# Moving all gate projections of a hybrid decoder layer from the final merge into the RWKV phase

## The chip, the core and the metric

The kernel runs on one core of one Trainium2 chip. The metric is the device time of one execution in microseconds. The core has a matrix engine (TensorE, PE in the profile; its weight loads are listed as PEld), VectorE (DVE), ScalarE (ACT), GpSimd (POOL) and a queue engine (SyncE, SP) that issues most of the DMAs; ACT issues some too. The engines run their own instruction streams, each in a fixed order, and wait for each other by semaphores.

## The reference: what is computed

x is 2048 tokens of 1024 channels in float32; there is one layer and one sequence.

```
h = rms_norm(x, norm_pre)
proj = h @ w_in            # split into c_q, c_kv, k_rope | u_rwkv | g_q, g_k, g_v, g_lat | br_gate | merge_gate
y_mla  = mla_branch(...)   # causal softmax attention, 8 heads
y_rwkv = rwkv7_branch(...) # delta-rule recurrence, 8 heads of 64, in chunks
y_gla  = gla_branch(...)   # gated linear attention, 4 heads
ys     = stack([y_mla, y_rwkv, y_gla]) * silu(br_gate)          # (2048, 3, 512)
branch = einsum('bsnw,nwd->bsnd', ys, w_branch_out)             # (2048, 3, 1024)
merged = sum(sigmoid(merge_gate) * branch, over the 3 branches) # (2048, 1024)
x      = x + rms_norm(merged @ w_out, norm_post)
```

br_gate has 3 × 512 channels and merge_gate 3 × 1024. Together they are 4608 channels, or 36 tiles of 128, each a product of h with a 1024 × 128 slice of w_in. These 36 gate tiles are what the change moves. Gates 0 to 11 are br_gate (four tiles for each branch), gates 12 to 35 are merge_gate (eight for each branch).

## The kernel before

**Arithmetic.** Data lie with channels on the 128 partitions and tokens along the free side, in blocks of 512 tokens (`TB`), four blocks in all (`NB`). A large product in fp32 is made from three fast matmuls: each operand is split into a high part (a cast to fp32r) and a low part (the rest), and `mm3` (lines 133 to 140) adds high·high, high·low and low·high into PSUM. One output tile of 128 channels by 512 tokens from 1024 inputs thus takes 8 × 3 = 24 matmuls. A weight comes as four loads of 128 KB; each load is split by a cast on ACT (line 121) and a subtraction on POOL (line 122), in `load_w` and `split`.

**RWKV phase** (`phase_rwkv`, line 331). For each block the kernel normalises x, transposes it into h (high and low, 16 tiles in a single buffer) and projects from it. The recurrence is cut into 16 stages (two channel groups × two half blocks × four blocks). A stage has a triangular solve on VectorE with round trips through DRAM (`within`), a preparation (`prepare`), and a chain of four chunk steps (`chain`) in which TensorE, VectorE and ACT alternate. The projections are filler for TensorE between these steps: `project_group` issues, for each half of a block's channels, its RWKV tiles (13 a block, `mixed`) and the tiles that the two other mixers need later (12 a block, `plain`, which go to the DRAM tensor `more` by `Plain.run`, lines 309 to 321). `mm3` records its matmuls in a list while `k.filling` is set, and `place` (line 142) ties the steps of `prepare` and `chain` to positions spread evenly over that list.

The instructions of each engine are ordered by a planner that simulates the program. Its priorities are program positions; `tc.high_priority(offset=PRI)` and its like put the recurrence ahead of the filler by so many instructions (`PRI` for chain and preparation, `PRI_W` for the solve, `PRI_O` for the operands, `PRI_H` for the next block's h).

**The fourth block's gates.** The last two stages have no later block to project. There `spare` (lines 1460 to 1464) makes all 36 gate tiles of the fourth block from its h, with a priority far behind everything (`PRI_LOW`), and stores them to the DRAM tensor `early`. They also fill TensorE while the GLA phase runs.

**GLA and MLA phases** (`phase_gla`, `phase_mla`) read `more`, and write y_g and y_m to DRAM; y_r is written by the RWKV phase.

**Merge** (`phase_merge`, line 1250). It goes through two halves of 1024 tokens. For each half it loads x again, normalises it with the known factors and transposes it into h (only the first 512 tokens in the second half, since the gates of the fourth block are known). For each of the three branches, in the order MLA, RWKV, GLA, it then projects the four br_gate tiles, forms y · silu(gate) and splits it into `yh` and `yl` (line 1312); and for each pair of output tiles it projects the merge_gate tiles, multiplies `yh`/`yl` by w_branch_out into `psb`, and adds tanh-gated results into `mg` (lines 1337 and 1340). The gate weights are loaded and split in each half anew. At the end comes the product with w_out and the last norm, 16 row tiles of 128 tokens, with the w_out halves in the places of h.

The lines that change in the merge are these two kinds of projection:

```
                    w = gate(n * 4 + i)
...
                            pre = project(b, w)
...
                        w = gate(12 + n * 8 + d)
...
                            pre = th if known(b) else project(b, w)
```

Of the kernel before, what the change touches and what calls it, by code (L numbers as in the profile page):

```python
# [9 lines left out]
F32 = mybir.dt.float32  # L10
F32R = mybir.dt.float32r
# [7 lines left out]
S = 2048  # L19
D = 1024  # L20
# [301 lines left out]
PRI = 1500  # L322
PRI_W = 500
# [3 lines left out]
PRI_O = 500  # L327
# [3 lines left out]
def phase_rwkv(k, pl, x, pos, w_rwkv, w_up2, w_more, y_dram, more, rope_dram, spare):  # L331
# [4 lines left out]
    with ExitStack() as st:  # L336
# [46 lines left out]
        def plain(B, h, ns):  # L383
            sl = slice(B * TB, B * TB + TB)
            pl.run(h, [w_more[n_] for n_ in ns], [more[n_][:, sl] for n_ in ns])

# [326 lines left out]
        def project_group(i):  # L713
# [22 lines left out]
            m = w_more.shape[0] // 2  # L736
            if xs:
# [39 lines left out]
        for i in range(n):  # L777
# [470 lines left out]
XB = 3  # L1248
TH = 4
def phase_merge(k, x, ys, early, w_gate, w_br, w_o, n_post, out):  # L1250
# [5 lines left out]
    with ExitStack() as st:  # L1256
        pool = lambda name, bufs=1, **kw: st.enter_context(k.pool(name, bufs, **kw))
        hp = pool("me_h", side="right")
        xp = pool("me_x")
        wp = pool("me_w")  # L1260
        t1 = pool("me_t")
        per = pool("me_per")
        ps_m = pool("me_psm", 2, space=PSUM)
        ps_g = pool("me_psg", 3, space=PSUM)
        ps_b = pool("me_psb", 3, space=PSUM)
        npost = per.tile([128, D], F32, name="npost")
        mg = [per.tile([128, 8, T], F32, name=f"mg{u}") for u in range(S // T)]

        for half in range(S // T):
            t0 = half * T  # L1270

            def known(b):

                return t0 + b * TB == S - TB

            def project(b, w):
                ps = ps_g.tile([128, TB], F32, name="psg")
                k.project(ps, w, h, slice(b * TB, (b + 1) * TB))
                return ps
# [7 lines left out]
            if half == 0:  # L1287
                nc.scalar.dma_start(out=npost, in_=n_post)

            def gate(n):  # L1290
                return k.load_w8(wp, w_gate[n], 128, "w", parts=4, rb=3, hb=4)

            for n in range(3):
                yh = [per.tile([128, T], F32R, name=f"yh{i}") for i in range(4)]
                yl = [per.tile([128, T], F32R, name=f"yl{i}") for i in range(4)]
                for i in range(4):
                    w = gate(n * 4 + i)
                    yt = xp.tile([128, T], F32, name="h_x", bufs=XB)
                    nc.sync.dma_start(out=yt, in_=ys[n][i][:, t0:t0 + T])
                    for b in range(NT):  # L1300
                        sl = slice(b * TB, (b + 1) * TB)
                        if known(b):
                            pre = xp.tile([128, TB], F32, name="h_x", bufs=XB)
                            nc.sync.dma_start(out=pre, in_=early[n * 4 + i])
                        else:
                            pre = project(b, w)
                        th = t1.tile([128, TB], F32, name="th", bufs=TH)
                        nc.scalar.activation(out=th, in_=pre, func=AF.Tanh, scale=0.5)
                        nc.vector.scalar_tensor_tensor(out=th, in0=th, scalar=1.0, in1=pre, op0=ALU.add, op1=ALU.mult)
                        nc.vector.scalar_tensor_tensor(out=th, in0=th, scalar=0.5, in1=yt[:, sl], op0=ALU.mult,  # L1310
                                                       op1=ALU.mult)
                        k.split(yh[i][:, sl], yl[i][:, sl], th)

                for d0 in range(0, 8, 2):
                    gates = []
                    for d in (d0, d0 + 1):
# [174 lines left out]
```

## Time and profile before

| | |
|---|---|
| median of 3 runs | 3126.67 us (3118.32 to 3131.35) |
| the profiled execution | 3124.77 us, span 3123.0 us |
| mean granted TensorE clock | 0.969 |
| TensorE / VectorE / ACT / POOL busy | 95% / 58% / 44% / 52% |
| RWKV projections and other filler in the RWKV and GLA phases (`psd`) | 18.7 to 1506 us |
| transposes of the attention weights in MLA (`pst`, line 1177) | 1535 to 2068 us |
| gate projections in the merge (`psg`) | 2073 to 2930 us |
| product with w_out | 2940 to 3114 us |

The profile has a page, and views that cut the same trace by line, by tile, by wait and by time. Busy time of TensorE is the union of matmuls whose ends are modelled, and matmuls overlap; so a full TensorE is judged here by the number of matmuls in a stretch as well. PEclk is the granted share of its clock. In views that list groups, the columns are: line, engine, operation, output<-inputs, form, count | busy us, mean ns of one | idle time of the engine just before them, and what ended it.

### The profile page before, as it was taken

The page shows a single profiled execution, that of the slowest core. Times are in us where ns is not written, and L with a number is a line of the kernel's source. Part 1 is how long each engine was busy: PE and PEld are TensorE (multiplying, and loading weights), DVE is VectorE, ACT ScalarE, POOL GpSimd, SP SyncE. Part 2 cuts the span into 40 slices and gives each one's busy share as a digit, 9 for nine tenths or more (in the row PEclk, how much of TensorE's full clock was granted, in tenths as well). Part 3 has the DMA queues.
Part 4 walks back from the last instruction along what each step waited for, and adds up shares of the span by engine and source line. Part 5 has one row for each costly group of instructions (what it writes and reads, how often), then busy time and mean ns, then how long its engine had stood idle before and what let it go on. Part 6 is the DMA issues. An engine that isn't in the chain of part 4 may idle for free.

```text
span 3123.0 us, 53491 instructions
## 1 busy us (share of the span) xinstructions
PE 2967.1 (95%) x18048; PEld 2423.4 (78%) x18048; DVE 1801.9 (58%) x5194; ACT 1387.8 (44%) x3211; POOL 1620.0 (52%) x2198
## 2 busy tenths in 40 slices
PE   8899998999989998898999999989999999999998
PEld 6676776777767776666798998878888888888887
DVE  3668787686888745888588888861110103122443
ACT  3343433333334444566677777762222224334321
POOL 5745554564645556676545545433244446477422
PEclk9999999999989999889999999999999999999999
DMA  4323232323213333233200000142121213344322
GB/s 135 99 84 102 83 89 90 89 81 87 71 53 94 110 118 101 88 99 96 65 22 17 18 19 18 33 129 70 49 75 48 71 51 107 107 133 146 110 95 88
DMA packets 261091, 253.01 MB, mean 81 GB/s; under 512 B 75328, under 2 KB 228816, under 8 KB 260816
## 3 DMA queue, kind: packets, MB, share of 16 engines
q1 hardware_dynamic: 236048, 220.03, 23.6%
q10 hardware_dynamic: 24768, 29.55, 3.0%
q8 instruction: 143, 2.34, 0.3%
q14 instruction: 132, 1.08, 0.1%
HBM read 201.77 MB, written 47.71 MB: 80 GB/s over the span
## 4 chain that ended last, share of the span: by engine, by line
PE 77%; DVE 15%; DMA 4%; issue 2%; ACT 1%; POOL 1%; SPq 0%; DVEq 0%; ACTq 0%; POOLq 0%
PE psg L136 7%; PE psg L137 7%; PE psg L138 7%; PE psd L136 6%; PE psd L138 6%; PE psd L137 5%; PE pso L1199 4%; PE pst L1177 4%; PE psb L136 4%; PE psb L137 4%; PE psb L138 4%; PE pss L136 3%; PE pss L138 3%; PE pss L137 3%; DVE xtmp L443 2%
## 5 line engine op out<-in xcount | busy, mean ns | idle before, releaser
L122 POOL TENSOR_TENSOR w_lo<-w_raw,w_hi 128x256 fp32r<-128x256 f32 x832 | 642.2, 777 | 515.9 <-ACT w_hi L121 455.8
L138 PE MATMUL psd<-hh,w_lo 128*128 128x512 f32 x1088 | 452.0, 417 | 4.4 <-POOL w_lo L122 4.3
L136 PE MATMUL psd<-hh,w_hi 128*128 128x512 f32 x1088 | 452.2, 416 | 4.1 <-DVE carry L402 3.1
L137 PE MATMUL psd<-hl,w_hi 128*128 128x512 f32 x1088 | 440.6, 405 | 0.0
L121 ACT CAST w_hi<-w_raw 128x256 fp32r<-128x256 f32 x624 | 250.6, 405 | 380.3 <-PE psg L137 162.1
L136 PE MATMUL psg<-hh,w_hi 128*128 128x512 f32 x864 | 336.3, 391 | 0.0
L137 PE MATMUL psg<-hl,w_hi 128*128 128x512 f32 x864 | 336.2, 390 | 0.0
L138 PE MATMUL psg<-hh,w_lo 128*128 128x512 f32 x864 | 332.3, 390 | 0.4 <-POOL w_lo L122 0.4
L1162 POOL TENSOR_SCALAR P<-P,nm 128x1024 f32<-128x1024 f32 (+2 forms) x192 | 166.7, 879 | 193.4 <-DVE nm L1159 146.5
L138 PEld LDWEIGHTS psd<-hh,w_lo 128*128 128x128 f32 x1088 | 210.6, 194 | 57.5 <-POOL w_lo L122 8.7
L136 PEld LDWEIGHTS psd<-hh,w_hi 128*128 128x128 f32 x1088 | 210.7, 194 | 52.8 <-issue 7.5
L137 PEld LDWEIGHTS psd<-hl,w_hi 128*128 128x128 f32 x1088 | 210.8, 194 | 43.2 <-issue 2.6
L1337 DVE SCALAR_TENSOR_TENSOR th<-th,psb 128x512 f32<-128x512 f32 x64 | 44.0, 687 | 341.1 <-PE psb L138 324.5
L1182 DVE TENSOR_TENSOR tl<-pst,th 128x512 fp32r<-128x512 f32 (+2 forms) x352 | 194.1, 562 | 29.9 <-ACT th L1181 28.4
L1181 ACT CAST th<-pst 128x512 fp32r<-128x512 f32 (+2 forms) x352 | 166.0, 489 | 78.4 <-PE pst L1177 39.4
L138 PEld LDWEIGHTS psg<-hh,w_lo 128*128 128x128 f32 x864 | 162.4, 188 | 34.3 <-POOL w_lo L122 0.8
L136 PEld LDWEIGHTS psg<-hh,w_hi 128*128 128x128 f32 x864 | 162.4, 188 | 34.1 <-ACT hh L231 0.3
L137 PEld LDWEIGHTS psg<-hl,w_hi 128*128 128x128 f32 x864 | 162.3, 188 | 33.4 <-DVE hl L232 0.2
L443 DVE TENSOR_TENSOR xtmp<-xm,xt 128x60 f32<-128x60 f32 (+24 forms) x496 | 155.0, 312 | 44.0 <-DMA xm<-dm 25.8
L1154 ACT ACTIVATE P<-P,nm 128x1024 f32<-128x1024 f32 (+2 forms) x192 | 172.3, 901 | 12.1 <-DVE nm L1150 11.8
L1140 DVE TENSOR_SCALAR_CACHE_REDUCE P<-pss 128x512 f32<-128x512 f32 (+3 forms) x288 | 168.4, 593 | 12.5 <-PE pss L138 9.1
L1177 PE MATMUL pst<-cs,P 128*128 128x128 f32 x1088 | 166.6, 275 | 1.1 <-DVE tl L1182 1.1
(395 smaller groups left out, 6935.4 us busy)
## 6 DMA issues: line engine op xcount, KB each, us to landing
w_raw<-in_w_gate_dram SPq DMA_DIRECT2D x432, 128.0 KB, 2.2
w_raw<-in_w_rwkv_dram SPq DMA_DIRECT2D x208, 128.0 KB, 2.2
w_raw<-in_w_more_dram SPq DMA_DIRECT2D x192, 128.0 KB, 2.2
h_x<-in_x_dram SPq DMA_DIRECT2D x40, 512.0 KB, 4.2
more<-plain SPq DMA_DIRECT2D x48, 256.0 KB, 2.6
wb_raw<-in_w_br_dram ACTq DMA_DIRECT2D x96, 128.0 KB, 2.1
early<-plain SPq DMA_DIRECT2D x36, 256.0 KB, 2.1
xm<-dm SPq DMA_DIRECT2D x64, 128.0 KB, 2.7
```

Source lines behind the costliest of these rows:

```text
L121: nc.scalar.copy(hi, src)
L122: (sub or nc.gpsimd).tensor_tensor(out=lo, in0=src, in1=hi.bitcast(F32), op=ALU.subtract)
L136: mm(out, lhsT=lhs[0], rhs=rhs[0], start=start, stop=False)
L137: mm(out, lhsT=lhs[0], rhs=rhs[1], start=False, stop=False)
L138: m = mm(out, lhsT=lhs[1], rhs=rhs[0], start=False, stop=stop)
L443: nc.vector.tensor_tensor(out=tv, in0=xm[:, j, j + 1:32].unsqueeze(1).broadcast_to([128, n2, n]), in1=xt[:, 0:n2, j:j + 1].broadcast_to([1 ...
L1140: nc.vector.tensor_scalar(out=pt[:, c0:c0 + f], in0=s_[:, 0:f], scalar1=-MLA_SCALE, scalar2=3e38, op0=ALU.mult, op1=ALU.min, accum_out=mx[ ...
L1154: nc.scalar.activation(out=pt[:, cw], in_=pt[:, cw], func=AF.Exp, bias=nm[:, 0:1], scale=-1.0, accum_out=nm[:, 1 + n:2 + n])
L1162: nc.gpsimd.tensor_scalar(out=pt[:, cw], in0=pt[:, cw], scalar1=nm[:, 1:2], scalar2=1.0, op0=ALU.mult, op1=ALU.mult)
L1177: nc.tensor.transpose(tp[:, kl, qt, :], P[qt][:, kt * 128:(kt + 1) * 128], k.ident)
L1181: nc.scalar.copy(flat(th)[:, r], flat(tp)[:, r])
L1182: nc.vector.tensor_tensor(out=flat(tl)[:, r], in0=flat(tp)[:, r], in1=flat(th)[:, r].bitcast(F32), op=ALU.subtract)
```

## The change

All 36 gate tiles of all four blocks are made in the RWKV phase. In `project_group`, for the first three blocks, `gates` makes 18 of them in each of the block's two groups, ahead of the `plain` tiles and inside the filler list; the fourth block's are made where `spare` made them. They go to a DRAM tensor `pre` of 36 × 128 × 2048. The priority offsets grow.

The merge has no h, no gate weights and no projection. It reads 1024 tokens of a gate tile from `pre` in one DMA of 512 KB: for the br_gates into the same ring as y (`h_x`, four buffers), for the merge_gates into a ring of its own (`h_g`, three buffers). The branches come in the order RWKV, GLA, MLA. `yh` and `yl` have two buffers each; half of their subtractions go to VectorE instead of POOL, and half of the sums into `mg` too. tanh of a merge_gate is one instruction for 1024 tokens. `psb` products use both PSUM pools, four banks each. The halves of w_out take the places of `yh`/`yl`, and the row tiles of the last product have places of their own (`mh`, `ml`).

```diff
-PRI = 1500
-PRI_W = 500
+PRI = 2400
+PRI_W = 1200
 PRI_H = 300
...
-PRI_O = 500
+PRI_O = 1200
...
+        def gates(B, h, ns):
+            for n_ in ns:
+                pl.run(h, [w_gate[n_]], [pre[n_][:, B * TB:B * TB + TB]])
...
             m = w_more.shape[0] // 2
+            half_g = w_gate.shape[0] // 2
+            if B < NB - 1:
+                gates(B, h, range(g * half_g, g * half_g + half_g))
...
-                spare(blk["h"])
+                with tc.high_priority(offset=-PRI_LOW):
+                    gates(NB - 1, blk["h"], range(w_gate.shape[0]))
...
-XB = 3
-TH = 4
+XB = 4
+XG = 3
+TH = 6
...
-            h = k.h_tiles(T, hp, "h")
-            if half == 0:
-                for o in range(0, T, 256):
-                    k.turn_h(k.norm_x(x, t0 + o, 2, xp, xbufs=XB), h, o, ((ps_m, "psm"),))
-            else:
-                rows = [mg[half][:, j, :] for j in range((T - TB) // 128)]
-                k.turn_h(k.norm_x(x, t0, len(rows), xp, into=rows), h, 0, ((ps_m, "psm"),))
...
-            for n in range(3):
-                yh = [per.tile([128, T], F32R, name=f"yh{i}") for i in range(4)]
+            for m_, n in enumerate((1, 2, 0)):
+                yh = [per.tile([128, T], F32R, name=f"yh{i}", bufs=2) for i in range(4)]
...
                     yt = xp.tile([128, T], F32, name="h_x", bufs=XB)
                     nc.sync.dma_start(out=yt, in_=ys[n][i][:, t0:t0 + T])
+                    gt = xp.tile([128, T], F32, name="h_x", bufs=XB)
+                    nc.sync.dma_start(out=gt, in_=pre[n * 4 + i][:, t0:t0 + T])
...
-                        nc.scalar.activation(out=th, in_=pre, func=AF.Tanh, scale=0.5)
-                        nc.vector.scalar_tensor_tensor(out=th, in0=th, scalar=1.0, in1=pre, op0=ALU.add, op1=ALU.mult)
+                        nc.scalar.activation(out=th, in_=gt[:, sl], func=AF.Tanh, scale=0.5)
+                        nc.vector.scalar_tensor_tensor(out=th, in0=th, scalar=1.0, in1=gt[:, sl], op0=ALU.add, op1=ALU.mult)
...
-                        k.split(yh[i][:, sl], yl[i][:, sl], th)
+                        k.split(yh[i][:, sl], yl[i][:, sl], th, nc.vector if i % 2 else None)
...
+                    gt = xp.tile([128, T], F32, name="h_g", bufs=XG)
+                    nc.sync.dma_start(out=gt, in_=pre[12 + n * 8 + d][:, t0:t0 + T])
+                    nc.scalar.activation(out=gt, in_=gt, func=AF.Tanh, scale=0.5)
...
-                        pb = ps_b.tile([128, TB], F32, name="psb")
+                        pb = (ps_b, ps_g)[turn % 2].tile([128, TB], F32, name=("psb", "psg")[turn % 2])
...
-                            nc.gpsimd.tensor_tensor(out=m, in0=m, in1=th, op=ALU.add)
+                            (nc.gpsimd, nc.vector)[b].tensor_tensor(out=m, in0=m, in1=th, op=ALU.add)
...
-        wo = k.h_tiles(D, hp, "h")
+        wo = [tuple(per.tile([128, D], F32R, name=f"y{m}{c % 4}", bufs=2) for m in "hl") for c in range(8)]
...
-            mh = per.tile([128, 8, 128], F32R, name=f"yh{j % 4}")
-            ml = per.tile([128, 8, 128], F32R, name=f"yl{j % 4}")
+            mh = hp.tile([128, 8, 128], F32R, name="mh", bufs=2)
+            ml = hp.tile([128, 8, 128], F32R, name="ml", bufs=2)
...
-    early = dp.tile([36, 128, TB], F32, name="early")
+    pre = dp.tile([36, 128, S], F32, name="pre")
```

More of the change, by code (lines that the diff above doesn't have):

```diff
@@ L326, with phase_rwkv @@
 NO = 3
-PRI_O = 500
+PRI_O = 1200
 C_DEC = -0.5 * math.exp(-0.5)
-def phase_rwkv(k, pl, x, pos, w_rwkv, w_up2, w_more, y_dram, more, rope_dram, spare):
+def phase_rwkv(k, pl, x, pos, w_rwkv, w_up2, w_more, w_gate, y_dram, more, pre, rope_dram):
     tc, nc = k.tc, k.nc
@@ L1247, in phase_mla, with phase_merge @@
             pass
-XB = 3
-TH = 4
-def phase_merge(k, x, ys, early, w_gate, w_br, w_o, n_post, out):
+XB = 4
+XG = 3
+TH = 6
+def phase_merge(k, x, ys, pre, w_br, w_o, n_post, out):
     tc, nc = k.tc, k.nc
@@ L1261, in phase_merge @@
         t1 = pool("me_t")
+        hp = pool("me_h")
         per = pool("me_per")
-        ps_m = pool("me_psm", 2, space=PSUM)
-        ps_g = pool("me_psg", 3, space=PSUM)
-        ps_b = pool("me_psb", 3, space=PSUM)
+        ps_g = pool("me_psg", 4, space=PSUM)
+        ps_b = pool("me_psb", 4, space=PSUM)
         npost = per.tile([128, D], F32, name="npost")
         mg = [per.tile([128, 8, T], F32, name=f"mg{u}") for u in range(S // T)]
+        nc.scalar.dma_start(out=npost, in_=n_post)
@@ L1269, in phase_merge @@
+        turn = 0
         for half in range(S // T):
             t0 = half * T
[L1272 to L1279, printed above, removed]
[L1280 to L1286 removed]
@@ L1287, in phase_merge @@
[L1287 to L1291, printed above, removed]
-            for n in range(3):
-                yh = [per.tile([128, T], F32R, name=f"yh{i}") for i in range(4)]
-                yl = [per.tile([128, T], F32R, name=f"yl{i}") for i in range(4)]
+            for m_, n in enumerate((1, 2, 0)):
+                yh = [per.tile([128, T], F32R, name=f"yh{i}", bufs=2) for i in range(4)]
+                yl = [per.tile([128, T], F32R, name=f"yl{i}", bufs=2) for i in range(4)]
@@ L1310, in phase_merge @@
                         nc.vector.scalar_tensor_tensor(out=th, in0=th, scalar=0.5, in1=yt[:, sl], op0=ALU.mult,
                                                        op1=ALU.mult)
-                        k.split(yh[i][:, sl], yl[i][:, sl], th)
-                for d0 in range(0, 8, 2):
-                    gates = []
-                    for d in (d0, d0 + 1):
-                        w = gate(12 + n * 8 + d)
-                        for b in range(NT):
-                            th = t1.tile([128, TB], F32, name="th", bufs=TH)
-                            if known(b):
-                                nc.sync.dma_start(out=th, in_=early[12 + n * 8 + d])
-                            pre = th if known(b) else project(b, w)
-                            nc.scalar.activation(out=th, in_=pre, func=AF.Tanh, scale=0.5)
-                            gates.append((d, b, th))
-                    for d, b, th in gates:
-                        if b == 0:
-                            wb = []
-                            for j in (0, 2):
-                                hi, lo = k.load_w(wp, w_br[n, d][:, j:j + 2, :], [128, 2, 128], "wb", rb=2, hb=3,
-                                                  eng=nc.scalar)
-                                wb += [(hi[:, i, :], lo[:, i, :]) for i in range(2)]
@@ L1332, in phase_merge @@
                         sl = slice(b * TB, (b + 1) * TB)
[L1333 removed]
+                        pb = (ps_b, ps_g)[turn % 2].tile([128, TB], F32, name=("psb", "psg")[turn % 2])
+                        turn += 1
                         for i in range(4):
                             k.mm3(pb, wb[i], (yh[i][:, sl], yl[i][:, sl]), i == 0, i == 3)
[L1336 to L1337 removed]
+                        m, th = mg[half][:, d, sl], gt[:, sl]
@@ L1458, in tile_hybrid_trunk @@
             pl = Plain(k, st)
-            def spare(h):
-                with tc.high_priority(offset=-PRI_LOW):
-                    for n in range(36):
-                        pl.run(h, [w_gate[n]], [early[n]])
-            phase_rwkv(k, pl, x, pos, w_rwkv, w_up2, w_more, y_r, more, rope, spare)
+            phase_rwkv(k, pl, x, pos, w_rwkv, w_up2, w_more, w_gate, y_r, more, pre, rope)
             hp = hand.enter_context(k.pool("hand", 1, side="right"))
@@ L1471, in tile_hybrid_trunk @@
         phase_mla(k, lat, rope, kr, w_uq, w_ukv, y_m)
-    phase_merge(k, x, (y_m, y_r, y_g), early, w_gate, w_br, w_o, n_post, out)
+    phase_merge(k, x, (y_m, y_r, y_g), pre, w_br, w_o, n_post, out)
 def kernel(**inputs):
```

19 lines of the change are left out of this document (9 added, 10 removed).

## The prediction

> **What bounds the kernel now.** I read the page's head first, to see which engine is full and where.
>
> ```profile
> span 3123.0 us, 53491 instructions
> PE 2967.1 (95%) x18048; PEld 2423.4 (78%) x18048; DVE 1801.9 (58%) x5194; ACT 1387.8 (44%) x3211; POOL 1620.0 (52%) x2198
> ...
> PE   8899998999989998898999999989999999999998
> ...
> PEclk9999999999989999889999999999999999999999
> ```
>
> TensorE is the bound, but its two eights and nines hide a difference between stages. So the second view is busy time by stage. I cut where the fourth block's gates begin (1076) and end (1510), at MLA's tail (2045), and at the merge's start and last stages.
>
> ```profile
> core 0: us, PE busy (x) PEld busy (x) DVE busy (x) ACT busy (x) POOL busy (x), PEclk, DMA share, GB/s
> ...
> 100.00:1076.00 976.00, 900.51 (x6019) 707.70 (x6018) 739.66 (x2213) 365.53 (x823) 534.22 (x810) 0.95 0.30 85
> 1076.00:1510.00 434.00, 395.61 (x3364) 298.69 (x3362) 308.27 (x748) 238.92 (x662) 274.29 (x463) 0.93 0.34 104
> ...
> 2045.00:2095.00 50.00, 38.47 (x242) 33.19 (x241) 32.78 (x68) 30.58 (x71) 11.25 (x14) 0.90 0.43 143
> 2095.00:2930.00 835.00, 834.59 (x3696) 690.46 (x3695) 152.25 (x199) 260.18 (x574) 420.41 (x483) 1.00 0.29 86
> 2930.00:2940.00 10.00, 9.13 (x40) 7.25 (x40) 6.07 (x6) 6.23 (x8) 2.72 (x2) 1.00 0.71 249
> 2940.00:3114.00 174.00, 173.90 (x767) 143.43 (x765) 72.64 (x230) 36.76 (x79) 42.50 (x32) 1.00 0.27 96
> ```
>
> The merge (2095 to 3114) is TensorE and nothing else: no idle time and a granted clock of 1.00. The RWKV stage (100 to 1076) loses 976 − 900.5 = 75.5 us to waits, and at a clock of 0.95 another 0.05 × 976 = 49 us. So 124 us of slack lie in the stage that receives the work. The third view says what the waits are.
>
> ```profile
> engine line waited for: us in total, times, longest us
> PE psu L532 <- DVE rhs L528: 19.6, 9, 5.7
> PE psa L523 <- DVE zbd L512: 9.6, 3, 5.8
> PE psm L422 <- DVE xtmp L443: 8.5, 2, 6.9
> PE psq L464 <- DVE yo L580: 4.4, 4, 1.4
> ```
>
> They are steps of the recurrence that reached TensorE before VectorE had their operand, not a lack of filler data.
>
> **The moved matmuls, at full rate: zero.** A gate tile of 512 tokens is 8 × 3 = 24 matmuls.
>
> ```profile
> L136 PE MATMUL psg<-hh,w_hi x864: 387/389/797, 2072.8 to 2929.8; 128*128 128x512 f32 x173
> ...
> L136 PE MATMUL psd<-hh,w_hi x1088: 387/389/988, 18.7 to 1505.8; 128*128 128x512 f32 x182
> ...
> 2500.00:2600.00 100.00, 100.00 (x443) 82.81 (x442) 8.99 (x13) 22.61 (x51) 43.04 (x50) 1.00 0.16 51
> ```
>
> The merge's projections are 3 × 864 = 2592 matmuls, that is 36 gates × 3 blocks × 24; the fourth block's are already among the `psd` ones. Back to back one takes 100 us / 442 = 0.226 us (the 389 ns overlap). So 586 us leave the merge, and 586 us at the same rate arrive in the RWKV stage. The forecast rests on what surrounds them.
>
> **What else each moved tile issues.** 108 tiles enter the RWKV loop, each with four weight loads and one store on SP's queue, four casts and one copy on ACT, four subtractions on POOL. The merge loses 288 weight loads with their splits, the RWKV stage gains 432.
>
> ```profile
> L138 PE MATMUL psd<-hh,w_lo 128*128 128x512 f32 x713 | 297.3, 419 | 1.5 <-POOL w_lo L122 1.4
> L122 POOL TENSOR_TENSOR w_lo<-w_raw,w_hi 128x256 fp32r<-128x256 f32 x357 | 276.8, 780 | 161.3 <-ACT w_hi L121 131.6 <-PE psd L138 11.6 <-PE psd L137 4.5
> L121 ACT CAST w_hi<-w_raw 128x256 fp32r<-128x256 f32 x177 | 70.7, 404 | 83.3 <-PE psd L137 48.2 <-POOL w_lo L122 15.9 <-issue 8.8
> L320 ACT COPY plain<-psd 128x512 f32<-128x512 f32 x45 | 26.3, 584 | 20.5 <-PE psd L138 15.6 <-DMA more<-plain 4.5
> ```
>
> POOL gets 432 × 0.780 = 337 us on top of 534, ACT 432 × 0.404 + 108 × 0.584 = 238 us on top of 366, VectorE nothing. In a stage of about 976 + 586 − 54 = 1508 us these are 58%, 40% and 49%: no new bound. One split feeds six matmuls (1.36 us), POOL needs 0.78 of them; TensorE waits 1.4 us for `w_lo` in the whole stage now. I cost them at nothing; the cover is the 0.58 us per split by which POOL is ahead. If the recurrence's own POOL work eats it, the filler stalls (second slow rival below). The same SP queue carries `dm`, `xm`, `dx` and `tt` of the triangular solve; five SP instructions per 5.4 us of TensorE work are the density that the present filler has too.
>
> **RWKV stage: −54 us.** Between two steps of the recurrence the program puts equal shares of the filler. A block has 25 filler tiles now and 61 after, for the same 4 × 15 steps: 25 × 5.43 / 60 = 2.3 us between steps becomes 5.5 us. The longest waits above are 5.7, 5.8 and 6.9 us, most are near 2, so the extra 3.2 us covers most but not all. I take 60% of the 75.5 (−45) and 60% of the clock's 49 (−29), since half-clock stretches follow the waits. Against it: a `psd` matmul beside small matmuls reads 419 ns where the merge's read 389, so alternating now costs 2141 × 0.030 = 64 us at most. Steps that now follow each other directly will be split by filler; I take a third, +20. Bounds: all slack gone, −124; or the new filler is slowed like the old, 586 / (0.923 × 0.95) − 586 = +82. I am nearer the first because the waits are for VectorE, whose load does not grow.
>
> On the clock the Trainium skill (TensorE: Matmul & The Clock Gate, § Part 1: The HAM clock gate) says that the array falls to half rate after an idle window of about 3.4 us and returns after one busy window. By that rule waits cut below 3.4 us give back the whole 49 us and not 60%, and the sum would end 20 us lower; the 0.95 in the row says only that the loss is there.
>
> **Merge.** It no longer normalises and transposes x.
>
> ```profile
> L226 PE MATMUL psm<-cs,h_x 128*128 128x128 f32 x56 | 10.0, 310 | 7.5 <-DVE hl L232 3.8 <-DVE h_x L205 3.6
> L226 PE MATMUL psm<-cs,mg 128*128 128x128 f32 x32 | 5.1, 272 | 0.0
> ...
> L1309 DVE SCALAR_TENSOR_TENSOR th<-th,h_x 128x512 f32<-128x512 f32 x12 | 11.4, 954 | 0.0
> L1310 DVE SCALAR_TENSOR_TENSOR th<-th,h_x 128x512 f32<-128x512 f32 x47 | 45.3, 981 | 0.9
> L1337 DVE SCALAR_TENSOR_TENSOR th<-th,psb 128x512 f32<-128x512 f32 x61 | 41.9, 687 | 341.1 <-PE psb L138 324.5 <-ACT th L1323 16.2 <-PE psm L226 0.4
> L1340 POOL TENSOR_TENSOR mg<-mg,th 128x512 f32<-128x512 f32 x61 | 78.7, 1292 | 37.3 <-DVE th L1337 29.7 <-PE psg L138 3.3 <-PE psb L137 2.0
> L122 POOL TENSOR_TENSOR yl<-th,yh 128x512 fp32r<-128x512 f32 x47 | 62.4, 1334 | 20.8 <-ACT yh L121 19.3
> L122 POOL TENSOR_TENSOR wb_lo<-wb_raw,wb_hi 128x256 fp32r<-128x256 f32 x92 | 68.3, 743 | 89.8 <-ACT wb_hi L121 63.5 <-PE psb L138 22.1 <-PE psb L137 3.3
> L122 DVE TENSOR_TENSOR hl<-h_x,hh 128x1024 fp32r<-128x1024 f32 x3 | 4.0, 1376 | 0.8 <-ACT hh L121 0.8
> L121 ACT CAST hh<-h_x 128x1024 fp32r<-128x1024 f32 x3 | 3.0, 1053 | 0.8 <-PE psg L138 0.8
> ```
>
> The transposes go: −10, between 0 (those before 2073 lie inside MLA) and −15.
>
> What remains of one branch in one half is 8 × 2 × 12 = 192 matmuls, 43.4 us. In it VectorE has eight gatings of 0.954 + 0.981, four subtractions and eight sums of about 0.69 (half of the 1376 ns row) and sixteen evictions of 0.687: 15.5 + 2.8 + 5.5 + 11.0 = 34.8 us. POOL has 16 × 0.743 + 4 × 1.334 + 8 × 1.292 = 27.6. Both fit, VectorE with 20% to spare and in order, so a gating may hold an eviction; eight PSUM banks (21 us of matmuls) cover that. Without this cover it costs a gating at each of five later branches: 5 × 1.9, taken as +8, between 0 and +15.
>
> The start (2045 to 2095) loses 50 − 38.5 + 0.10 × 50 = 16.5 us now, to transposes that wait. After, it waits for the first branch's gating instead, 8 × 1.94 = 15.5 us on VectorE, partly inside MLA's tail: 0, between −15 and +15.
>
> The end: four of the eight `w_o` pairs now take the last branch's `yh`/`yl` places, so their splits start when its last matmul is done: 1.05 + 4 × 1.38 = 6.6 us, of which the other four pairs cover 12 × 0.226 = 2.7: +4, between 0 and +7.
>
> **Sum**, against the profiled run's 3124.8 us (span 3123.0 and 1.8 around it; the runs' median of 3126.7 is 2 us above): −45 − 29 + 20 − 10 + 8 + 0 + 4 = −52, so 3073 for that run and 3075 for a median.
>
> **Rivals.**
>
> *All slack is used* (17%). All waits and half-clock stretches go and nothing is added by alternation: −124 − 10 + 12, 3003. For it: VectorE falls to 49%. Against: the waits come in bursts, when the solve's chain (`xtmp`) is in VectorE's queue.
>
> *The waits move along* (15%). If a step waits because VectorE's order has it behind the solve, wider spacing shifts the wait and does not shorten it. Then only −10 + 12 remains: 3127, no change. For it: the `xtmp` wait of 6.9 us. Against: 2.3 us of spacing is short of most waits.
>
> *The merge is starved* (14%, slower). This is a wait in place of the removed work, in the merge's loads on SP's queue.
>
> ```profile
> w_raw<-in_w_gate_dram SPq DMA_DIRECT2D x432, 128.0 KB, 2.2
> h_x<-in_x_dram SPq DMA_DIRECT2D x40, 512.0 KB, 4.2
> early<-plain SPq DMA_DIRECT2D x36, 256.0 KB, 2.1
> wb_raw<-in_w_br_dram ACTq DMA_DIRECT2D x96, 128.0 KB, 2.1
> ```
>
> A branch of a half now reads 16 tiles of 512 KB and 16 of 128 KB, 10.5 MB per 43.4 us, or 242 GB/s; the merge does 86 now. The best stretch shown is 249 GB/s at a DMA share of 0.71, so the queues can carry it, if at least two 512 KB loads are in flight: one alone gives 512 KB / 4.2 us = 125 GB/s, 84 us per branch and 6 × 41 = +243. It decides below two in flight on average, since a full buffer ahead in SP's order holds up all behind it. At 1.4 in flight, 175 GB/s, 60 us: 6 × 16.6 = +99 on the forecast, about 3172. Against it: seven buffers (four `h_x`, three `h_g`).
>
> The Trainium skill (DMA: Bandwidth & Descriptors, § Bandwidth) asks for at least 1 MiB per DMA to get 75% of the peak. These loads are half of that and need 0.69 of the 350 GB/s that the 0.71 row implies; by that rule this rival would come true in its mild form.
>
> *The filler is slowed like the old* (9%, slower). The +82 bound: weight splits late behind the recurrence's POOL work, with a price of 586 × 14%: 3125 + 82 + 2 = 3209. For it: 131.6 us in which POOL already waits for `w_hi`. Against: 1.4 us of TensorE waiting.
>
> **Chances.** The forecast has 45% with its own range of 3035 to 3105. About 0.5% (16 us) is what a measurement of this kernel can tell from no change. Faster: 45 + 17 + 2 of the middle case = 64%; within 0.5%: 13%; slower: 14 + 9 = 23%. The range for 8 in 10 runs from 3000, which leaves out half of the first rival, to 3155, which leaves out most of the slow ones.
>
> **What would show it.** Step by step: the RWKV stage ends near 1076 + 586 − 54 = 1608; the waits for `rhs`, `zbd` and `xtmp` fall from 38 us to below 16 and the granted clock of the stage rises to about 0.98; `psd` matmuls number 3 × 1952 and TensorE's wait for `w_lo` stays at a few us; the merge's stretch from the first `psb` to the end is near 450 us, with its DMA rate at 200 GB/s or more and a TensorE busy share of 97%. The forecast is wrong if the merge's TensorE has idle time that ends on `h_x` or `h_g` loads (starved), if the stage's waits stay near 75 us (moved along), or if `psd` matmuls wait for `w_lo` or `w_raw` (slowed filler).

## The result, and the profile after

The changed kernel takes 3144.06 us (median of four runs, 3143.02 to 3151.36). The kernel before took 3125.83 us in the runs beside it. The ratio is 1.0065, with a 95% interval of 1.0039 to 1.0091: the change makes the kernel slower by 0.65%, just beyond the 0.5% that the prediction counts as no change, which the interval still includes. The forecast was 3075 us.

The head of the page after: busy time and instructions of each engine, then the span in 40 equal slices, and one of its costliest groups.

```profile
span 3142.2 us, 54465 instructions
...
PE 2980.6 (95%) x17952; PEld 2399.4 (76%) x17952; DVE 1869.3 (59%) x5198; ACT 1473.5 (47%) x3375; POOL 1671.6 (53%) x2286
...
PE   8999989999999999998999988899999999999998
...
DVE  3613337813336814336976479867888888876443
...
L136 PE MATMUL psd<-hh,w_hi 128*128 128x512 f32 x1952 | 808.4, 415 | 13.3 <-DVE carry L406 7.1
```

TensorE's share is still 95%. The row to look at is VectorE's. In slices 1 to 20, most of the RWKV stage (a slice is 79 us), its digits go 3 6 1, 3 3 3 7 8, 1 3 3 3 6 8, 1 4 3 3 6 9: one or two slices at 60% or more in each block, and slices at 10 to 40% between. Before the change the same row was even. The RWKV stage ends there in slice 16, the last block's filler in slice 14, and from slice 2 to 14 no digit is below 6:

```profile
DVE  3668787686888745888588888861110103122443
```

Where the time went is read stage by stage, before and after, in windows cut at the same events of each kernel: the last store of `more`, the last `psa` matmul of the recurrence, MLA's first and last `pst` transposes, the end. The columns are the stretch, its length, and then busy time and instructions of TensorE, its weight loads, VectorE, ScalarE and GpSimd, the granted clock, DMA share and GB/s. First the kernel before:

```profile
100.00:1061.60 961.60, 891.78 (x5976) 701.08 (x5974) 727.38 (x2173) 361.17 (x811) 526.45 (x796) 0.95 0.30 86
1061.60:1187.00 125.40, 117.26 (x774) 91.58 (x773) 67.44 (x177) 54.94 (x134) 65.01 (x98) 0.96 0.37 114
1187.00:1534.80 347.80, 309.70 (x2735) 233.29 (x2733) 263.31 (x644) 199.97 (x572) 229.52 (x393) 0.90 0.31 95
1534.80:2067.80 533.00, 527.20 (x3609) 474.75 (x3608) 452.27 (x1617) 416.46 (x933) 269.30 (x294) 1.00 0.10 26
2067.80:3123.00 1055.20, 1036.39 (x4591) 855.67 (x4589) 250.16 (x478) 314.98 (x686) 468.16 (x519) 0.99 0.29 91
```

And the kernel after:

```profile
100.00:1656.70 1556.70, 1486.98 (x8470) 1164.95 (x8469) 757.95 (x2133) 582.34 (x1333) 835.53 (x1216) 0.97 0.36 108
1656.70:1797.80 141.10, 132.23 (x896) 103.83 (x896) 82.02 (x213) 63.27 (x153) 74.16 (x114) 0.96 0.36 111
1797.80:2146.90 349.10, 308.94 (x2705) 231.21 (x2703) 263.10 (x644) 197.69 (x566) 228.56 (x388) 0.89 0.29 92
2146.90:2677.50 530.60, 522.57 (x3578) 471.01 (x3577) 448.73 (x1609) 415.57 (x924) 267.31 (x291) 1.00 0.11 32
2677.50:3142.20 464.70, 444.89 (x1935) 361.16 (x1932) 275.16 (x490) 173.11 (x319) 204.01 (x178) 0.99 0.49 166
```

| stretch | before, us | after, us | difference, us |
|---|---|---|---|
| RWKV, to the last matmul of the recurrence (rows 1 and 2) | 1087.0 | 1697.8 | +610.8 |
| rest of GLA | 347.8 | 349.1 | +1.3 |
| MLA | 533.0 | 530.6 | −2.4 |
| merge and last product | 1055.2 | 464.7 | −590.5 |
| sum | 3023.0 | 3042.2 | +19.2 |

The merge gave back 590.5 us, somewhat more than the forecast's 586 for its matmuls. The RWKV stage took 610.8 for receiving them. It holds 8470 + 896 − 5976 − 774 = 2616 more matmuls; at the forecast's 0.226 us each they are 591 us. TensorE's idle time there was 1087.0 − 891.78 − 117.26 = 78.0 us and is 1697.8 − 1486.98 − 132.23 = 78.6: not one microsecond of the waits was used up. What the lower clock costs at most, half of every interval at half clock in the trace, added up instead of taken from the rounded rows, went from 52.9 to 47.8 us. 591 + 1 − 5 is 587, so 24 of the 610.8 are left. I put them down to alternating, for which 20 were forecast, but no run isolates it.

The waits themselves changed their names. TensorE's waits in the first window, the longest sums first (us in total, times, longest):

```profile
PE psm L426 <- DVE xt L449: 17.4, 4, 7.3
PE psd L136 <- DVE carry L406: 7.1, 2, 5.2
PE psq L479 <- DVE xh L477: 7.1, 3, 5.5
PE ps L661 <- ACT ta L626: 6.5, 4, 3.2
PE psd L138 <- POOL w_lo L122: 5.0, 9, 1.1
...
PE psu L536 <- DVE rhs L532: 2.8, 2, 2.4
...
PE psa L527 <- DVE zbd L516: 1.5, 1, 1.5
```

The recurrence's waits for `rhs` and `zbd`, 23.5 us in this window before, are down to 4.3. In their place TensorE waits for the end of the triangular solve (`xt`, at most 6.9 us at a time for its partner `xtmp` before, now 7.3) and for small VectorE steps. Of the 69.7 us idle in this window, 31.6 are the first three rows, all of them VectorE's.

Windows of 50 and 100 us show where that happens:

```profile
400.00:450.00 50.00, 49.09 (x275) 38.66 (x274) 11.60 (x29) 18.57 (x41) 24.45 (x36) 1.00 0.37 116
450.00:500.00 50.00, 38.37 (x185) 28.45 (x184) 31.89 (x59) 16.03 (x30) 32.36 (x46) 0.90 0.41 121
...
500.00:600.00 100.00, 91.29 (x485) 68.20 (x484) 81.02 (x238) 42.68 (x96) 55.30 (x76) 0.95 0.31 90
600.00:700.00 100.00, 100.00 (x583) 80.03 (x583) 33.60 (x102) 38.13 (x91) 47.67 (x68) 0.99 0.43 130
...
1400.00:1500.00 100.00, 84.00 (x454) 63.93 (x454) 68.62 (x194) 29.18 (x62) 55.04 (x89) 0.81 0.18 51
1500.00:1600.00 100.00, 93.61 (x576) 71.16 (x575) 85.09 (x253) 38.81 (x90) 53.55 (x78) 0.98 0.31 85
```

Where VectorE is at 23 and 34% (400 to 450, 600 to 700), TensorE is full or nearly so at a clock of 0.99 to 1.00. Where VectorE is at 64 to 85%, TensorE loses 6 to 23% of the time and the clock falls, down to 0.81. VectorE's mean over the stage did fall as the forecast said (757.95 of 1556.70 is 49%), but these windows lie far on both sides of it. Between 100 and 1800 us there are fifteen windows of 50 us in which VectorE is busy for 30 us or more; in them TensorE loses 68.8 of its 78.6 us.

The bursts are not the triangular solve alone. In 400 to 500 us, where TensorE loses 12.6 us, the solve's tile has a single instruction (shown below): VectorE has the operands, small steps and a table for MLA to do, and TensorE waits 5.2 us for `carry`, which frees the filler's PSUM bank, 3.2 for an ACT step of the operands (`ta`) and 3.0 for `mr`. In the whole stage VectorE is busy in 66.0 of the 78.6 idle us, and on the solve's tile in 23.7 of them.

The merge does what was forecast. In a stretch within it:

```profile
2700.00:2970.00 270.00, 261.69 (x1128) 211.66 (x1129) 185.59 (x228) 125.32 (x216) 153.71 (x140) 0.99 0.65 217
```

TensorE is 97% busy while the DMA engines move 217 GB/s, and its waits in the whole merge name no load:

```profile
PE psb L138 <- POOL wb_lo L122: 5.2, 6, 2.3
PE psb L136 <- ACT wb_hi L121: 3.9, 5, 1.5
PE psb L136 <- ACT yh L121: 1.1, 1, 1.1
```

### The profile page after: what moved, and what is told of

Its sections match the earlier page's. It is cut to its first block, busy times and chain, and to the rows that moved or that the text cites. A ratio compares the mean times of both kernels' runs of the same rounds, so it can differ in the third digit from the quotient of the medians.

```text
span 3142.2 us, 54465 instructions
## 1 busy us (share of the span) xinstructions
PE 2980.6 (95%) x17952; PEld 2399.4 (76%) x17952; DVE 1869.3 (59%) x5198; ACT 1473.5 (47%) x3375; POOL 1671.6 (53%) x2286
## 5 line engine op out<-in xcount | busy, mean ns | idle before, releaser
L136 PE MATMUL psd<-hh,w_hi 128*128 128x512 f32 x1952 | 808.4, 415 | 13.3 <-DVE carry L406 7.1
L138 PE MATMUL psd<-hh,w_lo 128*128 128x512 f32 x1952 | 791.8, 407 | 5.9 <-POOL w_lo L122 5.4
L137 PE MATMUL psd<-hl,w_hi 128*128 128x512 f32 x1952 | 777.3, 398 | 0.0
L136 PEld LDWEIGHTS psd<-hh,w_hi 128*128 128x128 f32 x1952 | 373.3, 191 | 105.6 <-issue 14.5
L138 PEld LDWEIGHTS psd<-hh,w_lo 128*128 128x128 f32 x1952 | 373.6, 191 | 101.8 <-POOL w_lo L122 17.4
L137 PEld LDWEIGHTS psd<-hl,w_hi 128*128 128x128 f32 x1952 | 373.8, 191 | 71.8 <-issue 3.2
L1163 ACT ACTIVATE P<-P,nm 128x1024 f32<-128x1024 f32 (+2 forms) x192 | 172.3, 902 | 11.9 <-DVE nm L1159 11.5
L449 DVE TENSOR_TENSOR xt<-xt,xtmp 128x60 f32<-128x60 f32 (+24 forms) x496 | 163.4, 330 | 13.5
L1208 PE MATMUL pso<-th,v 128*128 128x256 f32 x576 | 150.5, 284 | 0.8 <-DVE yo L1216 0.8
L1208 PE MATMUL pso<-tl,v 128*64 128x256 f32 x576 | 140.0, 283 | 4.7 <-DVE tl L1191 4.5
L1186 PEld LDWEIGHTS pst<-cs,P 128*128 128x128 f32 x1088 | 125.7, 141 | 11.9 <-DVE tl L1191 3.6
```

Of the source, the lines that this page charges most:

```text
L136: mm(out, lhsT=lhs[0], rhs=rhs[0], start=start, stop=False)
L137: mm(out, lhsT=lhs[0], rhs=rhs[1], start=False, stop=False)
L138: m = mm(out, lhsT=lhs[1], rhs=rhs[0], start=False, stop=stop)
L1163: nc.scalar.activation(out=pt[:, cw], in_=pt[:, cw], func=AF.Exp, bias=nm[:, 0:1], scale=-1.0, accum_out=nm[:, 1 + n:2 + n])
L1186: nc.tensor.transpose(tp[:, kl, qt, :], P[qt][:, kt * 128:(kt + 1) * 128], k.ident)
L1208: nc.tensor.matmul(d_, lhsT=l_, rhs=r_, start=kt == 0 and j == 0, stop=last and kl == 1 and j == 1)
```

## The experiments

All ran beside the kernel before (medians of 3122.45 to 3126.80 us). In the table, "RWKV" is the stretch from 100 us to the last matmul of the recurrence in the profiled run.

| kernel | median, us | ratio to before, 95% | RWKV, us |
|---|---|---|---|
| after the change | 3144.06 | 1.0065 (1.0039 to 1.0091) | 1697.8 |
| old_offsets | 3145.70 | 1.0064 (1.0040 to 1.0088) | 1702.5 |
| late_turn | 3145.78 | 1.0066 (1.0042 to 1.0090) | 1698.5 |
| operands_first | 3121.81 | 0.9988 (0.9976 to 1.0000) | 1676.6 |
| before_operands_first | 3121.06 | 0.9985 (0.9972 to 0.9997) | 1072.8 |
| filler_for_last_block | 3164.94 | 1.0129 (1.0107 to 1.0150) | 1751.9 |
| after_short_solve | 3084.79 | 0.9863 (0.9844 to 0.9882) | 1629.5 |
| before_short_solve | 3065.35 | 0.9807 (0.9788 to 0.9826) | 1021.6 |
| spread_solves | 3103.89 | 0.9933 (0.9920 to 0.9946) | 1658.5 |
| spread_late_start | 3111.28 | 0.9958 (0.9944 to 0.9973) | 1667.5 |
| spread_six_for_last | 3115.81 | 0.9973 (0.9959 to 0.9987) | 1684.1 |

**Why the solves come in bursts: three theories.** The program makes operands for stage i + 3 (`make(i + 3)`) behind the next block's `project_group`, whose last part turns the next h (`turned`). Both use the one PSUM bank `ps1`. The chart of VectorE says that something holds these operands until the block's filler is nearly done, and then two or three solves follow each other. It could be the larger priority offsets; it could be that the first transpose takes the bank early and holds it, until h's one buffer is free; or it could be the order in which the program hands the bank out, whenever the transposes run.

*old_offsets* puts the three offsets back:

```diff
-PRI = 2400
-PRI_W = 1200
+PRI = 1500
+PRI_W = 500
...
-PRI_O = 1200
+PRI_O = 500
```

> Edit: after, with PRI, PRI_W and PRI_O as before (1500, 500, 500). Theory P (the larger offsets pull the triangular solves together and so cause VectorE's bursts at 450 to 600, 900 to 1100 and 1400 to 1650 us): the bursts spread, the waits of the stage fall to about 45 us and the time to about 3115. Theory O: the bursts come from the operands' place in the program, the offsets matter little, 3130 to 3160.

Nothing moved: 3145.70 against 3144.06, and the RWKV stage is 5 us longer, not shorter. The offsets are not the cause.

*late_turn* keeps the first transpose off the bank until all but the last 16 entries of the filler (two tiles) are through:

```diff
-                    blk["h"] = turned(xs, (ps_1, "ps1"))
+                    blk["h"] = turned(xs, (ps_1, "ps1"), late=k.filling[:-16])
...
+                        if late and c == 0:
+                            self.place(m, late, len(late) - 1)
```

> Edit: after, with the first transposes of the next block's h held back to the last two filler tiles of the block, so that the PSUM bank ps1 is no longer held by a waiting transpose for 128 us in each of three blocks. Theory H (a held bank starves the recurrence): the operands that share ps1 come earlier, the waits of the RWKV stage fall from 70 us to about 40, time about 3105 to 3120. Theory O (the ring of ps1 is handed out in program order, and the odd stage's operands stand behind all of the next h's transposes in the program, so they cannot be early however late the transposes are): no change, 3140 to 3150, and the first matmul of the odd operands stays after the last transpose.

The edit did what it says and the time did not change. The transposes (L226) and the first matmuls of the next operands (L622, L624) around 300 to 460 us, after the change; the columns are count, shortest, median and longest ns, first and last start:

```profile
L226 PE MATMUL ps<-cs,h_x x32: 270/272/328, 300.1 to 452.1; 128*128 128x128 f32 x32
L622 PE MATMUL ps<-lwla,wup x8: 376/376/481, 454.2 to 457.1; 64*128 64x256 f32 x8
```

and in late_turn:

```profile
L226 PE MATMUL ps<-cs,h_x x32: 270/272/328, 424.1 to 451.7; 128*128 128x128 f32 x32
L624 PE MATMUL ps<-lwla,wup x8: 376/376/480, 453.8 to 456.7; 64*128 64x256 f32 x8
```

The transposes start 124 us later, so none of them holds the bank in that time, and yet the operands still start 2 us behind the last transpose. It is not the holding of the bank; the operands stand behind the transposes in the program's order for it, and the transposes end only once the filler has let go of h. After the change, the first transposed tile is written into h at 427.7 us, behind a filler matmul:

```profile
427.71 0.69 ACT L231 ACTIVATE hh<-ps,pc 128x512 fp32r<-128x512 f32 x1 [0.91 <-PE psd L138]
```

The added filler moved that moment back.

*operands_first* turns this order round and nothing else:

```diff
             if B < NB - 1:
+                if xs:
+                    make(2 * i + 1)
                 gates(B, h, range(g * half_g, g * half_g + half_g))
```

> Edit: after, with the operands of the odd stage made ahead of the gates and so ahead of the next h's transposes in the program (two of three blocks' halves gain, the first half of each block keeps its order). Theory O: the odd operands come 20 filler tiles (about 110 us) earlier, the solves come in pairs and not in threes, the waits of the RWKV stage from 100 us to its last store fall from 70 us to 40 to 50 and the time to 3105 to 3125. Theory L (what keeps the slack is the last block, which got no filler, so the waits at 1400 to 1656 stay and the others move): 3135 to 3150. Theories H and P expect no more than 10 us.

```profile
L226 PE MATMUL ps<-cs,h_x x32: 271/272/329, 324.4 to 464.2; 128*128 128x128 f32 x32
L622 PE MATMUL ps<-lwla,wup x8: 376/376/480, 298.6 to 303.5; 64*128 64x256 f32 x8
```

The operands now start at 298.6 instead of 454.2, and the kernel takes 3121.81 us: 22 us less than after the change, level with before. The order of these operands is a cause. The waits in the first window fell less than expected, from 69.7 to 61.8 us and not to 40 to 50; the clock's loss fell from 42.7 to 29.0.

*before_operands_first* makes the same edit in the kernel before:

```diff
             if xs:
+                make(2 * i + 1)
                 for j in range(m, 2 * m - 2):
```

> Edit: before, with the odd stage's operands made ahead of the next h's transposes, as in the run with the operands first. Theory O says that the ring's order costs before little, since its transposes and the odd operands lie 4 filler tiles (about 25 us) apart and not 22: 3115 to 3130, no change. If the order costs both kernels the same, it is no cause of the difference between them: about 24 us faster, 3102.

It gains 5 us there (0.9985, 0.9972 to 0.9997), little more than the noise, against 22 in the kernel after. The order was in the code all along, and cost little as long as a block had 25 filler tiles.

**What the solves cost in both kernels.** The short-solve kernels leave out part of the computation: 30 of the 31 steps of each triangular solve.

```diff
-            for j in range(31):
+            for j in range(1):
```

> Edit: after, with one of the 31 steps of each triangular solve (the output is not the reference's; 960 VectorE instructions, some 300 us of VectorE's time, are left out). Theory B: the bursts go, the waits of the RWKV stage fall from 70 us to below 25, and the time by 60 to 90 us, to about 3070. Theory N or a wait on something else than VectorE: 3110 or more.

> Edit: before, with one of the 31 steps of each triangular solve (the output is not the reference's). It is the pair of the run above: the same work less, in a stage without the gates. Theory B says that the slack which the prediction meant to fill is VectorE's solve in both kernels: before falls by 60 to 90 us too, to about 3050, and stays ahead or level with the run above. If before falls by less than 40 us, its waits were latency of the chain, which filler could have covered.

Both fall by about 60 us (3144.06 to 3084.79, and 3126.80 to 3065.35), and the changed one stays 19 us behind by the medians, 11.5 in the profiled runs (3074.68 and 3063.21). Their stages, after_short_solve first:

```profile
100.00:1617.80 1517.80, 1477.86 (x8612) 1164.52 (x8610) 518.28 (x1287) 596.10 (x1363) 854.10 (x1238) 0.99 0.37 111
```

```profile
100.00:1011.20 911.20, 876.94 (x6030) 689.25 (x6029) 522.58 (x1296) 369.00 (x826) 535.51 (x805) 0.97 0.32 91
```

VectorE's load falls by about 30%, TensorE's idle time from about 70 to 40 and 34 us, the clock rises. So the solve is worth some 60 us in both kernels, and the change left all of that in place. The waits did not fall below 25 us as expected: other steps keep TensorE waiting for 40. It also follows that the 24 us put down to alternation do not come from the solves: without them the stage still grows by 1629.5 − 1021.6 = 607.9 us, where its 2594 more matmuls are 586; waits account for 6 of the difference, and the clock's loss is 9 lower.

**Spreading the solves.** If the bursts hold the slack, then solves at even distances must give the forecast's gain to the changed kernel. *spread_solves* makes the operands halfway through the gates of a group, behind the filler recorded so far, and puts the start of each solve (the first `psm` matmul of `within`) at a fixed place in the filler:

```diff
...
-                gates(B, h, range(g * half_g, g * half_g + half_g))
+                c = g * half_g
+                gates(B, h, range(c, c + half_g // 2))
+                if i > 0:
+                    make(2 * i + 1, list(k.filling))
+                gates(B, h, range(c + half_g // 2, c + half_g))
...
-        def stage_w(i):
+        def stage_w(i, fill=None):
             if i < n:
+                f = int(len(fill or ()) / 2 * (i % 2 + 0.3))
                 with tc.high_priority(offset=PRI_W):
-                    W[i] = G[i], *within(i, G[i])
+                    W[i] = G[i], *within(i, G[i], lambda m: k.place(m, fill, f))
...
-            stage_w(i + 2)
+            stage_w(i + 2, fill)
```

> Edit: after, with the odd stage's operands made halfway through the gates and bound to that place, and with the first matmuls of each triangular solve bound to 0.3 of the half of the filler in which the stage two ahead is due. So the solves come about one per half group and not in twos or threes. Theory B (bunched solves on VectorE, not a lack of filler, keep TensorE waiting in the blocks that have filler): the waits from 100 us to the last store of more fall from 70 us after, and 62 with the operands first, to about 40, the time to 3095 to 3112, below both kernels. Theory N (any order gives some 60 us of waits, since the solve's matmuls wait for VectorE wherever they stand): 3118 to 3130, as with the operands first.

It takes 3103.89 us: 40 less than after the change, and 0.67% less than before (0.9933, 0.9920 to 0.9946). Of the kernels here that leave nothing out it is the fastest. VectorE's and GpSimd's work on `xt`, the solves' tile, in windows of 100 us: in the kernel before,

```profile
300.00:400.00 100.00, 30.23 (x103) 0.40 (x1) 0.97 0.27 79
400.00:500.00 100.00, 26.93 (x94) 0.80 (x2) 1.00 0.34 97
500.00:600.00 100.00, 33.59 (x114) 0.80 (x2) 0.93 0.32 92
```

after the change,

```profile
300.00:400.00 100.00, 19.86 (x62) 0.40 (x1) 1.00 0.42 125
400.00:500.00 100.00, 0.24 (x1) 0.00 (x0) 0.95 0.39 118
500.00:600.00 100.00, 39.95 (x124) 0.89 (x1) 0.95 0.31 90
```

and with the solves spread:

```profile
300.00:400.00 100.00, 21.44 (x68) 0.40 (x1) 1.00 0.42 122
400.00:500.00 100.00, 17.64 (x57) 0.40 (x1) 0.97 0.41 126
500.00:600.00 100.00, 19.52 (x62) 0.40 (x1) 1.00 0.36 108
```

A solve is 62 of these instructions. Before, they came evenly, some 100 per 100 us; after the change there were 62, none, and 124; spread, there are about 60 in each. And the stage:

```profile
100.00:1625.00 1525.00, 1471.54 (x8484) 1151.91 (x8483) 762.98 (x2133) 580.35 (x1333) 829.92 (x1216) 0.99 0.36 110
```

TensorE's idle time is 53.5 us in place of 69.7, and the clock's loss, summed as above, 17.1 in place of 42.7. Together that is 42 us less than after the change. Against the kernel before, from which the forecast counted its 74, it is 47: the waits fell from 69.8 to 53.5 us, 16 where 45 were forecast, and the clock's loss from 47.8 to 17.1, 31 where 29 were forecast. The time fell as theory B has it, the waits less: 53.5 us, not about 40. Between 450 and 500 us TensorE still loses 6.6 us, without an instruction on `xt`.

**Filler for the last block.** The change gives 36 gates to each of the first three blocks. The fourth keeps the 25 tiles it had, since its own gates cover GLA, and after the change its stretch is the worst (1400 to 1500, above). *filler_for_last_block* is operands_first with half of these gates moved forward:

```diff
+            elif g == 0:
+                gates(B, h, range(half_g))
...
-                    gates(NB - 1, blk["h"], range(w_gate.shape[0]))
+                    gates(NB - 1, blk["h"], range(w_gate.shape[0] // 2, w_gate.shape[0]))
```

> Edit: the run with the operands first, and 18 of the fourth block's 36 gate tiles in the RWKV filler of that block's first group instead of the filler of low priority that reaches into GLA. Theory L: the last block's stretch (256 us for 132 filler matmuls per 50 us, 22 us of waits and a clock of 0.92) loses 25 to 35 us of its slack; GLA loses half of its filler, which costs it nothing where VectorE bounds it: about 25 us below the run with the operands first. Theory O alone: what the last block gains GLA gives back, within 10 us of that run.

```profile
100.00:1760.50 1660.50, 1594.73 (x9065) 1247.02 (x9064) 803.76 (x2233) 634.73 (x1458) 900.94 (x1310) 0.98 0.37 110
...
1851.90:2165.00 313.10, 237.29 (x2381) 173.60 (x2380) 244.78 (x644) 176.12 (x499) 186.91 (x335) 0.81 0.22 69
```

It loses 43 us against operands_first; neither theory expected that. RWKV grows from 1676.6 to 1751.9, by 75, for 18 tiles that are 98 us of matmuls, and GLA shrinks only from 346.5 to 313.1 us, by 33, since 75.8 of its 313 us are now idle at a clock of 0.81: the moved tiles were GLA's own cover. *spread_six_for_last* tries a third of the dose on spread_solves (`gates(B, h, range(6))` there):

> Edit: the run with the solves spread, and 6 of the fourth block's 36 gate tiles in the filler of that block's first group (18 were tried before). Theory L: the stretch of 1400 to 1600 us, the only one that still waits for 20 us, is covered by 33 us of filler, and GLA with 30 tiles loses less than that: 5 to 15 us below 3104. Theory G (GLA pays for each tile that it lacks with most of its 5.4 us): 3104 to 3125.

```profile
1784.10:2118.70 334.60, 282.16 (x2602) 207.64 (x2601) 261.81 (x644) 189.82 (x545) 218.33 (x372) 0.88 0.28 86
```

That is GLA, with 52.4 us idle where spread_solves has 37.0 (345.20 us, 308.23 of them busy). The kernel takes 3115.81 us, 12 more than spread_solves; their ratios to the kernel before, 0.9973 and 0.9933, have intervals that do not meet. Even six tiles of cover are worth more in GLA than in the last block.

*spread_late_start* lets the recurrence begin sooner: it puts all 36 gates of the first block into that block's second group.

```diff
-                gates(B, h, range(c, c + half_g // 2))
+                ns = range(c, c + half_g) if B else range(2 * c)
+                gates(B, h, ns[:len(ns) // 2])
...
-                gates(B, h, range(c + half_g // 2, c + half_g))
+                gates(B, h, ns[len(ns) // 2:])
```

> Edit: the run with the solves spread, and all 36 gate tiles of the first block in its second group, so that the first chain starts at about 110 us and not at 227. Theory S (the recurrence starts 118 us later after the change than before it, its backlog is carried to the end and shows in the 16 us longer tail behind the last store of more): 10 to 20 us below 3104. Theory E (chain steps are tied to the filler of their own group, so a late start is made up in the next group): within 6 us of 3104.

3111.28 us, not faster than spread_solves (0.9958 against 0.9933, and the RWKV stage 9 us longer), though its first `psa` matmul comes at 107.3 us in place of 225.6. So the late start by itself is not what the changed kernel pays for; that the gates moved for it cost something in the second group is not excluded.

## Why the prediction was wrong, point by point

**Sign and size.** Forecast 3075, measured 3144. The range of 3000 to 3155 held it by 11 us, the likeliest case's own (3035 to 3105) did not, and slower had only 23%.

**The moved matmuls, at full rate: zero.** Right: 36 × 3 gates left the merge and arrived in the RWKV stage, the group quoted counts 1952 `psd` matmuls of its kind, and the merge's 590.5 us against RWKV's 591 us of matmuls cancel.

**What else each moved tile issues, at nothing.** Right: TensorE waits 5.0 us for `w_lo` in the RWKV window and no load appears among its long waits. The slowed-filler rival did not come.

**RWKV stage: −54 us.** This is the step that failed, in its two gains. The waits were to give −45 and gave +1; the clock was to give −29 and gave −5; the alternation was to cost +20, and what is left over is about +24. The sum of the step is +20 in place of −54, and that alone turns the result. That 24 lies near 20 is luck. The bound of 64 us behind the 20 compared a mean of 419 ns, which contains matmuls at half the clock, with a stretch that has none. Outside the half-clock intervals the `psd` matmuls of that stage take 405 ns on average and those of the merge 389.5, which gives 2141 × 0.016 = 34 us and a third of 11; the rest was counted under the clock already.

The reasoning behind it had two faults. It took "equal shares" between the recurrence's steps as if waits were set by a step's distance from the one before, 2.3 us to 5.5 us. For `rhs` and `zbd` that was right: they fell as forecast, 23.5 to 4.3 us. But what stood behind the sum of the waits was VectorE busy with the solves, the operands and small steps, and the forecast argued that VectorE's load doesn't grow, from a mean over the stage. (It grew a little, from 794.8 us for 2350 instructions to 840.0 for 2346.) The load went from evenly spread to bunched, because more filler in a block pushes back the moment at which h is released, and with it the transposes and everything behind them in the order of bank `ps1`. late_turn shows the order, operands_first and spread_solves show the cost: 22 and 40 us. How much of it belongs to the solves and how much to the operands that move with them, the runs do not separate. The prediction named `turned` nowhere in its steps; a moved tile that reads h also moves the release of h.

With the solves spread, waits and clock give 47 of the forecast's 74 us: the clock's share about as forecast, the waits' a third of it. That kernel's 3103.89 lies at the edge of the likeliest case's own range, but it has two edits that the forecast did not have, and so confirms nothing of it.

The second fault: 61 tiles were counted for all four blocks. The last keeps 25, so a quarter of the old stage got no filler to gain from: of the 69.7 us idle after the change, 22.4 lie between 1400 and 1600 us. The two kernels that gave it more lost more in GLA than it gained.

**Merge: +2 for its extras.** Right within 7 us as a sum: it fell by 590.5 where 584 was forecast (586 − 2). Its parts were not measured one by one. VectorE was to have a fifth to spare and is busy 185.59 of 270 us, 69%. The stretch from the first `psb` matmul to the end, forecast at near 450 us, is 461 us.

**The rivals.** "The waits move along" came true in the sum, 78.0 to 78.6 us idle, though its price of 3127 lacked the alternation. "All slack is used" named the reason against itself that decided: waits come in bursts when the solve's chain is in VectorE's queue. I gave that no term. "The merge is starved" did not come: 217 GB/s against a need worked out as 242, no idle time of TensorE on `h_x` or `h_g`. The Trainium skill (DMA: Bandwidth & Descriptors, § Bandwidth) asks for at least 1 MiB per DMA for 75% of the peak; the 512 KB loads here ran at a DMA share of 0.65 and TensorE did not wait for them, so that rule did not decide.

**What the signs said.** `rhs`, `zbd` and `xtmp` did fall under 16 us (to 11.5 over the whole stage, while `xt`, the last step of the same solve, took 17.4), and that sign alone would have passed the step as right. The RWKV stage's sum (78.6 us idle, "near 75") passed it as wrong. A sign that names single waits can't test a claim on their sum.

**What stays open.** Where the 24 us put down to alternation come from; they are there without the solves too. The solves were not spread in the kernel before, so its 3126.80 us against 3103.89 compare an untuned order with a tuned one; before_operands_first, at 3121.06, is the nearest pair there is. And with spread_solves 53.5 us of idle time remain in the first window; the edits that added cover to its last block or changed its start only made it worse.

## What to carry to other kernels

In this kernel filler covered waits only where the waited-for engine's work was spread as evenly as the filler: look at that engine in windows of a block's length, not at its mean over a stage. When work is moved into a loop, ask which buffer it reads holds up, what is queued behind that buffer's release (here transposes, and behind these, in one bank's program order, the operands of the next solve), and put the bound engine's suppliers ahead of it. State the test of a wait argument as the sum of idle time, since single waits rename themselves.

## What was not expected of the hardware

The clock falls without a long wait. In the kernel before, the 3.4 us ahead of a stretch at half clock, and that stretch, twice:

```profile
964.70:968.10 3.40, 1.50 (x10) 1.29 (x11) 3.01 (x11) 0.48 (x2) 2.33 (x4) 1.00 0.37 112
968.10:971.50 3.40, 3.40 (x10) 2.66 (x9) 2.09 (x7) 1.98 (x5) 1.26 (x3) 0.50 0.52 119
1169.60:1173.00 3.40, 1.51 (x7) 1.12 (x8) 3.21 (x9) 2.53 (x7) 3.31 (x7) 0.99 0.36 98
1173.00:1176.00 3.00, 3.00 (x8) 2.32 (x7) 2.15 (x3) 0.99 (x3) 1.56 (x2) 0.50 0.15 46
```

TensorE had run 1.50 and 1.51 us of the 3.4, and its longest single gap was 1.4 and 1.8 us. So it was a thin stretch that brought the half clock, not one long wait; in both VectorE is busy nearly throughout (3.01 and 3.21 of 3.40 us). The trace of the kernel before has 17 such falls in its RWKV stage, and in the 3.4 us ahead of 11 of them no gap of TensorE reaches 3 us (in one of them, at 749.7 us, TensorE is busy throughout, mostly with small matmuls of 64*64 and 128*64); the others stand at gaps of 3.4 to 6.9 us. The prediction cited the Trainium skill (TensorE: Matmul & The Clock Gate, § Part 1: The HAM clock gate) for a fall after an idle window of about 3.4 us, and worked out that by that rule waits cut below 3.4 us give back the whole loss. These rows differ from that reading. It also fits that spread_solves gained more from the clock (26 us against the kernel after) than from the waits (16 us): thinning the bursts removes thin stretches whose waits were short. That was not tested by itself.
